# A layer step of a hybrid encoder on one core: the three shared projections loaded amid the modulation's weights and multiplied chunk by chunk

## The chip, the cores and the metric

The kernel runs on one core of a Trainium2 chip. The metric is device time in microseconds (us) of one execution. A core has a matrix engine, TensorE (PE; its weight loads are listed as PEld), VectorE (DVE), ScalarE (ACT), GpSimd (POOL) and SyncE (SP), whose queue (SPq) issues nearly all DMAs here. Each engine takes its instructions strictly in the order of its own queue; instructions of different engines wait for each other through semaphores.

## What is computed

One layer for two request groups that share weights: 256 prompt tokens and 8 x 16 sample tokens, 384 tokens of width 1024, in float32. The part that the change touches is the beginning:

```
mod = silu(c) @ w_ada + b_ada -> shift1, scale1, gate1, shift2, scale2, gate2   (per sequence, 9 sequences)
h   = RMSNorm(x) * (1 + scale1) + shift1
P   = h @ w_in        columns: [RWKV-7: r k v | wd ad gd] [attention: q k v qi ki wi] [two branch gates]
branch A: RWKV-7 time mixing on P (low-rank decay from tanh(wd), in-context rate from ad, gate from gd)
branch B: sparse attention with an indexer (qi, ki, wi) and top-k keys
m = sigmoid(gA) * (oA @ w_proj_a) + sigmoid(gB) * (oB @ w_proj_b);   x = x + gate1 * (m @ w_out)
h2 = RMSNorm(x) * (1 + scale2) + shift2;   x = x + gate2 * PEER(h2)     (product-key experts, 16,384 rows)
```

The "three shared projections" are the columns wd, ad and gd of w_in (96 to 128 columns each in the kernel's units wa, wb, wg): small inputs of the low-rank maps that all 16 RWKV heads share.

## The kernel before

The kernel is written with a tile framework: the program is traced in order, and a scheduler then lays down the order of every engine's queue from priorities (the order of tracing) and from a simulation of when each instruction's inputs are ready. Tiles come from pools; a pool that is opened in the memory of a closed one waits for the closed pool's readers. A tag with `bufs=n` has n buffers in turn, and a new tile waits until the buffer's last reader is done. The context `issue_after(ins)` places what is traced inside it, on `ins`'s engine, behind `ins` in that engine's queue.

**Precision.** A product in float32 quality is made of three matmuls: each operand is split into a high half (ScalarE copies to a rounded type, line 230) and a low half (VectorE or GpSimd subtracts, line 234), and high x high, high x low and low x high are summed in PSUM. `wload` (243) loads a weight unit and splits it; `raw` (236) is the load into one of four buffers of tag "w"; the high halves "wh" have four buffers, the low halves "wl" three (`WB = (4, 4, 3)`).

**The front** (`run`, 1585 ff., first pool "ph"):

- `setup` and `mod_head` load small constants; `front_x` (445) normalises three tiles of 128 tokens and transposes them into xT (8 chunks of 128 features x 384 tokens).
- `front_h` (463) goes over the 8 chunks two at a time. For chunks c, c+1 it needs two modulation units, `mod_unit(c // 2)` (shift) and `mod_unit(c // 2 + 4)` (scale). A unit (383) is 256 columns of w_ada: two loads of 512 KB, half a unit each; the matmuls of a half appear as eight instructions "mm<-w,cst", four transposing steps as "bx<-cfirst,mr" after ScalarE's copy "mr". Then VectorE makes h1A (404), VectorE and ScalarE modulate (480 to 484), and h is split into LTh (485, 486) and LTl (487 on VectorE for the sample tokens, 488 on GpSimd for the prompt).
- The units are traced in the order 0, 4, 1, 5, 2, 6, 3, 7: 16 loads of 512 KB.
- Line 1602 then loads wa, wb and wg (`self.early`) into buffers of tag "w", and behind the last of them in SP's queue come the late constants: cfront, clate, crope, a row of norm weights (qkn), the rope tables rt made on GpSimd (343 to 352) and six stores that clear DRAM scratch from a tile "zero" (357 to 365).

**What follows.** `rwkv_head` (515, pool "rw") calls `shifted` (491) for wa, wb and wg: it splits the weight, makes the whole product in a PSUM bank of tag "mm" (two banks; `tposp`, 276: 8 chunks x 3 terms = 24 matmuls), copies it to SBUF (502, 503), mixes each token with its forerunner, and from the results come XW (525), XV and XG. Then the work follows the string `ORDER` (177): two gate units (G, 24 matmuls each), the indexer (`index`, which begins with ki, 24 matmuls and a transposition in a "dx" bank), more gate units, the eight RWKV pairs (R), the other modulation units (M) and the attention quarters (D). The first use of XW on PE is the pair's decay product at line 561 ("fx<-XW,wup").

PSUM has eight banks: tags mm 2, fx 2, bx 1, dx 2, cp 1 (`PSB`). Up to `rwkv_head` the dx and cp banks are unused.

Of the kernel before, what the change touches and what calls it, by code (L numbers as in the profile page):

```python
# [18 lines left out]
OP = mybir.AluOpType  # L19
# [8 lines left out]
NT = 384  # L28


UNITS = {"wa": (3072, 128), "wb": (3200, 128), "wg": (3328, 96)}
# [164 lines left out]
class K:  # L196
# [58 lines left out]

    def win(self, name):
        n = UNITS[name][1]
        return self.wload(self.win_ap(name), n, self.early.pop(name, None)), n

    def win_ap(self, name):  # L260
        n = UNITS[name][1]
# [201 lines left out]
    def front_h(self):  # L463

        nc = self.nc
        hi = self.t([128, 8, NT], F32R, tag="LTh", pool=self.hpool)
        lo = self.t([128, 8, NT], F32R, tag="LTl", pool=self.hpool)
        self.LT = (hi, lo)
        self.h1B = self.scT[:, 0]
        self.h1A = self.pool.tile([128, 8, 9], F32, name="h1A")  # L470
        h = self.xT
        for c in range(0, 8, 2):
            cs = slice(c, c + 2)
            self.mod_unit(c // 2)
            self.mod_unit(c // 2 + 4)
            self.mod_cols(cs)
            hs = h[:, cs, 0:128]
            o = hs.rearrange("p c (b t) -> p c b t", t=16)
            bc = lambda a: a[:, cs, :8].unsqueeze(3).to_broadcast([128, 2, 8, 16])
            nc.vector.tensor_tensor(o, o, bc(self.h1A), op=OP.mult)  # L480
            nc.vector.tensor_tensor(o, o, bc(self.h1B), op=OP.add)
            for cc in (c, c + 1):
                hp = h[:, cc, 128:NT]
                nc.scalar.activation(hp, hp, AF.Identity, scale=self.h1A[:, cc, 8:9], bias=self.h1B[:, cc, 8:9])
            nc.scalar.activation(hi[:, cs, 0:128], hs, AF.Copy)
            nc.vector.tensor_copy(hi[:, cs, 128:NT], h[:, cs, 128:NT])
            nc.vector.tensor_tensor(lo[:, cs, 0:128], hs, hi[:, cs, 0:128], op=OP.subtract)
            nc.gpsimd.tensor_tensor(lo[:, cs, 128:NT], h[:, cs, 128:NT], hi[:, cs, 128:NT], op=OP.subtract)  # L488


    def shifted(self, name, ch, tag, bufs=2):

        nc = self.nc
        W, m = self.win(name)
        pt = self.t([128, 393], tag="pt", bufs=2)
        X = self.t([128, NT], tag=tag, bufs=bufs)
        pts = pt[:m, 0:136].rearrange("p (b t) -> p b t", t=17)
        ptp = pt[:m, 136:393]
        nc.gpsimd.tensor_copy(pts[:, :, 0], self.shT[:m, :, ch])
        nc.gpsimd.memset(ptp[:, 0:1], 0.0)  # L500
        p = self.tposp(W, 0, m, self.LT)
        nc.scalar.activation(pts[:, :, 1:], p[:, 0:128].rearrange("p (b t) -> p b t", t=16), AF.Copy)
        nc.scalar.activation(ptp[:, 1:], p[:, 128:NT], AF.Copy)
        Xs = X[:m, 0:128].rearrange("p (b t) -> p b t", t=16)
        Xp = X[:m, 128:NT]
        nc.gpsimd.tensor_tensor(Xs, pts[:, :, 0:16], pts[:, :, 1:17], op=OP.subtract)
        nc.gpsimd.tensor_tensor(Xp, ptp[:, 0:256], ptp[:, 1:257], op=OP.subtract)
        mu = self.col["mu"][:m, ch:ch + 1]
        nc.vector.scalar_tensor_tensor(Xs, Xs, mu, pts[:, :, 1:17], op0=OP.mult, op1=OP.add)
        nc.vector.scalar_tensor_tensor(Xp, Xp, mu, ptp[:, 1:257], op0=OP.mult, op1=OP.add)  # L510
        nc.gpsimd.tensor_copy(self.last[:m, 0:8, ch], pts[:, :, 16])
        nc.gpsimd.tensor_copy(self.last[:m, 8, ch:ch + 1], ptp[:, 256:257])
        return X
# [1071 lines left out]
    def run(self):  # L1585
        hs = self.ctx.enter_context(ExitStack())
        self.halves = self.open(hs, "halves")
        with ExitStack() as front:
            fh = front.enter_context(ExitStack())
            self.fconst = self.open(fh, "fconst")  # L1590
            self.hpool = self.open(fh, "hpool")
            self.fill = self.open(fh, "fill")
            self.psum = self.open(self.ctx, "psum", space=bass.MemoryType.PSUM)
            self.lo_pattern = "v"
            with ExitStack() as s:
                self.pool = self.open(s, "ph")
                self.setup()
                self.mod_head()
                self.front_x()
                self.front_h()  # L1600

                self.early = {name: self.raw(self.win_ap(name)) for name in ("wa", "wb", "wg")}
                with self.tc.issue_after(self.wdma.ins):
                    self.load_consts("cfront", self.fconst)
                    self.setup_front()
            self.lo_pattern = "v"
            self.gd = self.dt_([16, 128, NT])
            self.oad, self.obd = self.dt_([128, 8, NT]), self.dt_([128, 8, NT])
            with ExitStack() as s:
                rw = self.open(s, "rw")  # L1610
                self.pool = rw
                self.rwkv_head()
                self.rw = rw
                ds, n = None, dict.fromkeys("RGD", 0) | {"M": 8}
                for x in ORDER:
                    if x == "I":
                        with ExitStack() as s2:
                            self.pool = self.open(s2, "idx", side="right")
                            self.index()
                        ds = self.open(s, "dsa", side="right")  # L1620
                        continue
                    if x in "123":
                        self.pick_s() if x == "1" else self.pick_p("23".index(x))
                        continue
                    self.pool = rw if x == "R" else ds
                    self.lo_pattern = "g" if x == "g" else "v"
                    x = x.upper()
                    {"R": self.rwkv_pair, "M": self.mod_unit, "G": self.gate_unit, "D": self.dsa_quarter}[x](n[x])
                    n[x] += 1
                self.nc.sync.dma_start(self.O["sh"], self.last)  # L1630
            fh.close()
            self.hpool2 = self.open(self.ctx, "hpool2", side="right")
            qs = self.ctx.enter_context(ExitStack())
            self.qpool = self.open(qs, "qpool", side="right")
            with ExitStack() as s:
                mixp = self.pool = self.open(s, "mixp")
                self.mix()
                self.scores_head()
                for u in range(4):
                    self.out_unit(u)  # L1640
                sel = self.sel = self.open(qs, "sel", side="right")
                for i in range(3):
                    self.h2_tile(i)
# [49 lines left out]
        with ExitStack() as s:  # L1693
# [3 lines left out]
            nc = self.nc  # L1697
# [52 lines left out]
```

## Time and profile before

| | us |
|---|---|
| median of 3 runs | 1776.21 (1772.17 to 1779.79) |
| the profiled execution | 1770.59 |
| its span, first to last instruction | 1768.8 |
| PE busy in the span | 1672.8 |
| DVE / ACT / POOL busy | 1360.3 / 749.7 / 553.4 |

The mean granted clock of TensorE was 0.983 of full speed. In rows of the timeline the first number is the start in us from the span's start, the second the duration; then engine, line, operation, output and inputs, shapes, count, and in brackets the idle time before it and what ended it. Rows of the chain are start, duration, what. Rows of a table of stretches ("A:B") give the length, each engine's busy time with its count of instructions (PE, PEld, DVE, ACT, POOL), the granted TensorE clock, the DMA engines' busy share and GB/s. Matmuls are pipelined and their ends are modelled: the distance of two starts is the price of one in a row of them.

### The profile page before, as it was taken

The page shows a single profiled execution, that of the slowest core. Times are in us where ns is not written, and L with a number is a line of the kernel's source. Part 1 is how long each engine was busy: PE and PEld are TensorE (multiplying, and loading weights), DVE is VectorE, ACT ScalarE, POOL GpSimd, SP SyncE. Part 2 cuts the span into 40 slices and gives each one's busy share as a digit, 9 for nine tenths or more (in the row PEclk, how much of TensorE's full clock was granted, in tenths as well). Part 3 has the DMA queues.
Part 4 walks back from the last instruction along what each step waited for, and adds up shares of the span by engine and source line. Part 5 has one row for each costly group of instructions (what it writes and reads, how often), then busy time and mean ns, then how long its engine had stood idle before and what let it go on. Part 6 is the DMA issues. An engine that isn't in the chain of part 4 may idle for free.

```text
span 1768.8 us, 33168 instructions
## 1 busy us (share of the span) xinstructions
PE 1672.8 (95%) x12424; PEld 1402.2 (79%) x12424; DVE 1360.3 (77%) x2902; ACT 749.7 (42%) x1652; POOL 553.4 (31%) x616
## 2 busy tenths in 40 slices
PE   6999899999999999998989889999989999999998
PEld 4988688778888877998878789999966667667766
DVE  3448878778867765555999999899867777877787
ACT  4433343334243333334233265577853333443344
POOL 1433343333342320024032223242243333333332
PEclk8999899999999999999999989999999999999999
DMA  8543662555364365755388989987559999999995
GB/s 301 161 123 103 185 194 67 153 175 153 94 215 140 105 204 191 235 189 185 125 333 323 342 302 389 374 330 263 192 203 393 342 367 363 374 356 390 344 382 215
DMA packets 172537, 436.71 MB, mean 247 GB/s; under 512 B 46036, under 2 KB 86100, under 8 KB 155992
## 3 DMA queue, kind: packets, MB, share of 16 engines
q1 hardware_dynamic: 153944, 300.36, 50.5%
q0 software_dynamic: 18432, 134.23, 19.9%
q8 instruction: 98, 1.61, 0.4%
q14 instruction: 63, 0.52, 0.1%
HBM read 403.23 MB, written 31.30 MB: 246 GB/s over the span
## 4 chain that ended last, share of the span: by engine, by line
PE 55%; DVE 19%; DMA 14%; issue 6%; ACT 3%; POOL 2%; SPq 1%; DVEq 0%; POOLq 0%; ACTq 0%
PE mm L226 20%; PE fx L226 13%; PE dx L226 9%; PE cp L226 6%; PE bx L226 5%; DMA w<-in_pv 3%; DMA raw<-in_puv,pe 3%; DVE wl L234 3%; DVE acc L1581 2%; DVE raw L1575 2%; DMA w<-in_puT 2%; ACT wh L230 1%; DMA w<-in_w_ada 1%; DMA w<-in_w_in 1%; DMA NL<-d 1%
## 5 line engine op out<-in xcount | busy, mean ns | idle before, releaser
L234 DVE TENSOR_TENSOR wl<-w,wh 128x1024 fp32r<-128x1024 f32 (+1 forms) x280 | 351.7, 1263 | 108.4 <-ACT wh L230 72.4
L230 ACT ACTIVATE wh<-w 128x1024 fp32r<-128x1024 f32 (+1 forms) x288 | 300.8, 1051 | 171.6 <-PE mm L226 77.2
L1568 POOL DMA_INDIRECT raw<-in_puv,pe x128 | 171.2, 1338 | 446.6 <-PE dx L226 156.5
L226 PE MATMUL fx<-h2h,wl 128*128 128x256 f32 x736 | 209.6, 285 | 8.8 <-DVE wl L234 8.8
L226 PE MATMUL fx<-h2h,wh 128*128 128x256 f32 x736 | 210.3, 286 | 3.0 <-ACT wh L230 2.8
L226 PE MATMUL fx<-h2l,wh 128*128 128x256 f32 x736 | 207.3, 282 | 0.0
L1581 DVE SCALAR_TENSOR_TENSOR acc<-raw,dots,acc 128x1024 f32<-128x1024 f32 x127 | 165.6, 1304 | 16.0 <-ACT dots L1577 15.7
L1575 DVE SCALAR_TENSOR_TENSOR raw<-raw,sh 128x1024 f32<-128x1024 f32 x128 | 160.3, 1252 | 7.7 <-DMA raw<-in_puv,pe 7.5
L226 PEld LDWEIGHTS fx<-h2h,wl 128*128 128x128 f32 x736 | 139.9, 190 | 12.5 <-DVE wl L234 12.1
L226 PEld LDWEIGHTS fx<-h2h,wh 128*128 128x128 f32 x736 | 139.9, 190 | 7.8 <-ACT wh L230 6.3
L226 PEld LDWEIGHTS fx<-h2l,wh 128*128 128x128 f32 x736 | 139.9, 190 | 1.7 <-issue 1.3
L226 PE MATMUL fx<-h2f,w 128*128 128x256 f32 x576 | 128.2, 382 | 11.5 <-ACT G L1484 11.5
L226 PEld LDWEIGHTS fx<-h2f,w 128*128 128x128 f32 x576 | 108.1, 190 | 29.7 <-ACT G L1484 14.9
L226 PE MATMUL mm<-LTh,wh 128*128 128x384 f32 (+2 forms) x352 | 123.2, 351 | 1.9 <-ACT wh L230 1.3
L226 PE MATMUL mm<-LTl,wh 128*128 128x384 f32 (+2 forms) x352 | 122.7, 349 | 0.5 <-POOL LTl L488 0.5
L226 PE MATMUL mm<-LTh,wl 128*128 128x384 f32 (+2 forms) x352 | 122.1, 347 | 0.0
L226 PE MATMUL mm<-wh,LTh 128*128 128x256 f32 x336 | 99.2, 296 | 2.9 <-ACT qx L888 2.9
L226 PE MATMUL mm<-wl,LTh 128*128 128x256 f32 x336 | 98.5, 293 | 0.0
L226 PE MATMUL mm<-wh,LTl 128*128 128x256 f32 x336 | 97.7, 291 | 0.0
L1576 ACT ACTIVATE dots<-dots 128x1 f32<-128x1 f32 x128 | 25.5, 199 | 161.7 <-DVE raw L1575 159.3
L226 PEld LDWEIGHTS mm<-LTh,wh 128*128 128x128 f32 (+2 forms) x352 | 66.2, 188 | 7.7 <-issue 3.0
L226 PEld LDWEIGHTS mm<-LTl,wh 128*128 128x128 f32 (+2 forms) x352 | 66.3, 188 | 3.2 <-issue 1.5
(571 smaller groups left out, 4152.3 us busy)
## 6 DMA issues: line engine op xcount, KB each, us to landing
w<-in_puT SPq DMA_DIRECT2D x128, 512.0 KB
w<-in_pv SPq DMA_DIRECT2D x128, 512.0 KB
w<-in_w_in SPq DMA_DIRECT2D x70, 512.0 KB
w<-in_w_ada SPq DMA_DIRECT2D x48, 512.0 KB
cKT<-in_cKT SPq DMA_DIRECT2D x32, 256.0 KB
cV<-in_cV SPq DMA_DIRECT2D x32, 256.0 KB
w<-in_w_pq SPq DMA_DIRECT2D x16, 512.0 KB
d<-wst SPq DMA_DIRECT2D x8, 832.0 KB
```

The costliest lines, as they stand in the source:

```text
L226: return self.nc.tensor.matmul(out, l, r, start=start, stop=stop, skip_group_check=True, **kw)
L230: self.nc.scalar.activation(hi, src, AF.Copy)
L234: (self.nc.vector if eng == "v" else self.nc.gpsimd).tensor_tensor(lo, src, hi, op=OP.subtract)
L1568: d = nc.gpsimd.indirect_dma_start(out=bass.AP(tensor=u.tensor, offset=u.offset, ap=[u.ap[0], [1, 2048]]), out_offset=None, in_=self.I["puv"],
L1575: nc.vector.scalar_tensor_tensor(u, u, 1.0, h2, op0=OP.mult, op1=OP.mult, accum_out=dot)
L1576: nc.scalar.activation(dot, dot, AF.Gelu_apprx_tanh)
L1581: nc.vector.scalar_tensor_tensor(acc, v, dot, acc, op0=OP.mult, op1=OP.add)
```

## The change

The three weights wa, wb and wg are loaded behind the fourth modulation unit traced (unit 5, the eighth w_ada load) instead of behind the sixteenth, into three tiles of their own in the first pool, and are split there. Their products go to the two dx banks and the cp bank, open from then on: the matmuls of chunks 0 to 3 are traced after chunks 2 and 3 of h are split, those of 4, 5 and of 6, 7 after theirs. `shifted` takes the finished bank. The late constants are placed behind the last w_ada load on SP's queue and, what of them runs on GpSimd, behind the last LTl of h. The number of matmuls, splits and loaded bytes stays.

```diff
--- before.py
+++ after.py
@@ -255,7 +255,7 @@
 
     def win(self, name):
         n = UNITS[name][1]
-        return self.wload(self.win_ap(name), n, self.early.pop(name, None)), n
+        return self.wload(self.win_ap(name), n), n
 
     def win_ap(self, name):
         n = UNITS[name][1]
@@ -469,10 +469,14 @@
         self.h1B = self.scT[:, 0]
         self.h1A = self.pool.tile([128, 8, 9], F32, name="h1A")
         h = self.xT
+        self.first = {}
         for c in range(0, 8, 2):
             cs = slice(c, c + 2)
             self.mod_unit(c // 2)
             self.mod_unit(c // 2 + 4)
+            if c == 2:
+                with self.tc.issue_after(self.wdma.ins):
+                    self.first_weights()
             self.mod_cols(cs)
             hs = h[:, cs, 0:128]
             o = hs.rearrange("p c (b t) -> p c b t", t=16)
@@ -485,20 +489,45 @@
             nc.scalar.activation(hi[:, cs, 0:128], hs, AF.Copy)
             nc.vector.tensor_copy(hi[:, cs, 128:NT], h[:, cs, 128:NT])
             nc.vector.tensor_tensor(lo[:, cs, 0:128], hs, hi[:, cs, 0:128], op=OP.subtract)
-            nc.gpsimd.tensor_tensor(lo[:, cs, 128:NT], h[:, cs, 128:NT], hi[:, cs, 128:NT], op=OP.subtract)
+            self.lolast = nc.gpsimd.tensor_tensor(lo[:, cs, 128:NT], h[:, cs, 128:NT], hi[:, cs, 128:NT], op=OP.subtract)
+            for name in ("wa", "wb", "wg"):
+                if c == 2:
+                    self.first_products(name, (0, 1, 2, 3))
+                elif c > 2:
+                    self.first_products(name, (c, c + 1))
+
+    def first_weights(self):
+
+        for name, tag in (("wa", "dx"), ("wb", "dx"), ("wg", "cp")):
+            n = UNITS[name][1]
+            w = self.t([128, 1024], tag="we" + name)[:, :8 * n].rearrange("p (k c) -> p k c", k=8)
+            self.nc.sync.dma_start(w, self.win_ap(name))
+            self.first[name] = (self.wload(None, n, w), n, self.ps([128, NT], tag=tag)[:n])
+
+    def first_products(self, name, ks):
+
+        W, n, p = self.first[name]
+        hi, lo = self.LT
+        for k in ks:
+            wh, wl = W(k)
+            self.mm(p, wh, hi[:, k], start=(k == 0), stop=False)
+            self.mm(p, wh, lo[:, k], start=False, stop=False)
+            self.mm(p, wl, hi[:, k], start=False, stop=(k == 7))
 
 
     def shifted(self, name, ch, tag, bufs=2):
 
         nc = self.nc
-        W, m = self.win(name)
+        m = UNITS[name][1]
+        if name not in self.first:
+            W, m = self.win(name)
         pt = self.t([128, 393], tag="pt", bufs=2)
         X = self.t([128, NT], tag=tag, bufs=bufs)
         pts = pt[:m, 0:136].rearrange("p (b t) -> p b t", t=17)
         ptp = pt[:m, 136:393]
         nc.gpsimd.tensor_copy(pts[:, :, 0], self.shT[:m, :, ch])
         nc.gpsimd.memset(ptp[:, 0:1], 0.0)
-        p = self.tposp(W, 0, m, self.LT)
+        p = self.first[name][2] if name in self.first else self.tposp(W, 0, m, self.LT)
         nc.scalar.activation(pts[:, :, 1:], p[:, 0:128].rearrange("p (b t) -> p b t", t=16), AF.Copy)
         nc.scalar.activation(ptp[:, 1:], p[:, 128:NT], AF.Copy)
         Xs = X[:m, 0:128].rearrange("p (b t) -> p b t", t=16)
@@ -1599,8 +1628,7 @@
                 self.front_x()
                 self.front_h()
 
-                self.early = {name: self.raw(self.win_ap(name)) for name in ("wa", "wb", "wg")}
-                with self.tc.issue_after(self.wdma.ins):
+                with self.tc.issue_after(self.wdma.ins), self.tc.issue_after(self.lolast.ins):
                     self.load_consts("cfront", self.fconst)
                     self.setup_front()
             self.lo_pattern = "v"
```

## The prediction

> **What bounds the kernel now.** I read the engines' share of the chain, then a table of stretches, then the chain of the first 60 us, then each engine's rows there.
>
> ```profile
> PE 55%; DVE 19%; DMA 14%; issue 6%; ACT 3%; POOL 2%; SPq 1%; DVEq 0%; POOLq 0%; ACTq 0%
> ...
> 0.00:55.00 55.00, 38.53 (x255) 26.75 (x256) 22.71 (x56) 24.09 (x47) 17.21 (x41) 0.84 0.88 297
> ...
> sum 1768.00, PE 1672.83 PEld 1402.19 DVE 1360.28 ACT 749.73 POOL 553.39; mean PE 152.08 PEld 127.47 DVE 123.66 ACT 68.16 POOL 50.31
> ```
>
> The first number of each group is the engine's busy time. TensorE (PE) idles 1768.00 - 1672.83 = 95.2 us in all, and 55.00 - 38.53 = 16.5 us of that lies in the first 55 us: 1/32 of the span holds a sixth of the idle time. The chain says what the PE waits for there.
>
> ```profile
> 28.61 4.84 DMA w<-in_w_ada
> ...
> 35.10 6.04 DMA cfront<-in_cfront
> ...
> 47.10 1.25 POOL LTl L488
> ...
> 48.39 2.02 PE mm L226 x10
> ...
> 50.99 8.61 PE mm L226 x48
> ```
>
> Up to 36 us it is the w_ada loads; then the constants' loads, which hold SP's queue; then the last chunk of h's low half on POOL. From 48.39 on the chain is PE matmuls almost without a break, so the start of the matmuls is what the change can move, and a shift of that start reaches the end as long as nothing downstream is rearranged. I take as mark the first matmul of the first gate unit, G0, the first that belongs to none of the three shared products:
>
> ```profile
> 17.85 0.61 PE L226 MATMUL bx<-cfirst,mr 128*128 128x9 f32 x4
> ...
> 21.60 0.64 PE L226 MATMUL mm<-w,cst 128*32 128x256 f32 x8 [0.93 <-DMA w<-in_w_ada]
> ...
> 31.30 1.02 PE L226 MATMUL bx<-cfirst,mr 128*128 128x9 f32 x4
> ...
> 36.24 1.08 PE L226 MATMUL mm<-w,cst 128*32 128x256 f32 x8 [0.61 <-DMA w<-in_w_ada]
> ...
> 38.61 0.69 PE L226 MATMUL mm<-LTh,wh 128*128 128x384 f32 x1 [1.29 <-ACT wh L230]
> ...
> 40.59 0.52 PE L226 MATMUL mm<-LTh,wh 128*128 128x384 f32 x1
> ...
> 40.91 0.52 PE L226 MATMUL mm<-LTl,wh 128*128 128x384 f32 x1
> ...
> 43.53 0.34 PE L226 MATMUL mm<-LTh,wl 128*128 128x384 f32 x1
> ...
> 43.70 0.34 PE L226 MATMUL mm<-LTh,wh 128*128 128x384 f32 x1
> ...
> 55.27 0.34 PE L226 MATMUL mm<-LTh,wh 128*128 128x384 f32 x1
> ...
> 59.52 0.92 PE L226 MATMUL fx<-XW,wup 64*128 64x384 f32 x4
> ```
>
> G0 starts at 55.27. The same rows give the prices of PE work at two clocks. A product matmul starts 0.32 us after its forerunner at 40.59 to 40.91 (cold) and 0.17 to 0.18 us at 43.53 to 43.70 (warm; I use 0.175). Half a modulation unit (one row "mm<-w,cst" x8) takes 0.64 warm, 1.08 cold; its transposing step (bx x4) 0.61 and 1.02. The row at 21.60 is the 8th half unit of 16, the one at 36.24 the 16th.
>
> **The change, part by part.** No matmul, split or byte is added or removed; 72 product matmuls (3 names, 8 chunks, 3 terms) and three loads change place.
>
> *The loads.* The three weights move from behind the 16th w_ada load to behind the 8th.
>
> ```profile
> 20.00:30.00 10.00, 6.61 (x68) 3.03 (x59) 3.08 (x10) 4.07 (x10) 2.76 (x2) 0.79 0.91 317
> 30.00:40.00 10.00, 7.84 (x54) 4.25 (x46) 4.54 (x9) 4.43 (x9) 1.26 (x1) 0.50 0.95 313
> ...
> w<-in_w_in SPq DMA_DIRECT2D x21, 512.0 KB
> w<-in_w_ada SPq DMA_DIRECT2D x16, 512.0 KB
> ...
> w<-in_w_in SPq DMA_DIRECT2D x1, 384.0 KB
> ```
>
> The last three numbers of a window are granted clock, DMA share and GB/s: the DMA engines are 91 to 95% busy, so bytes put in front delay what follows. wa and wb are 512 KB each, wg 384 KB (the one load of that size): 1.44 MB, at 315 GB/s 4.6 us. The 16th half unit, which waited for its load until 36.24, starts at 40.8. That is the cost. SP issues these loads without a buffer wait (they get tiles of their own), so the w_ada loads behind them stand only in the line of bytes.
>
> *The last chunk of h.* What is saved is seen by comparing the third chunk's chain with the last one's.
>
> ```profile
> 25.82 1.38 POOL L488 TENSOR_TENSOR LTl<-xT,LTh 128x512 fp32r<-128x512 f32 x1 [2.58 <-DVE LTh L486]
> ...
> 30.65 0.39 ACT L392 ACTIVATE mr<-mm 128x256 f32<-128x256 f32 x1 [2.95 <-PE mm L226]
> ...
> 34.42 1.26 POOL L488 TENSOR_TENSOR LTl<-xT,LTh 128x512 fp32r<-128x512 f32 x1 [7.21 <-DVE LTh L486]
> ...
> 38.47 0.37 ACT L392 ACTIVATE mr<-mm 128x256 f32<-128x256 f32 x1
> 38.59 2.51 DVE L234 TENSOR_TENSOR wl<-w,wh 128x1024 fp32r<-128x1024 f32 x2 [2.54 <-ACT wh L230]
> ...
> 42.72 0.16 DVE L404 SCALAR_TENSOR_TENSOR h1A<-scT,cols 128x18 f32<-128x18 f32 x1
> ...
> 43.89 3.21 POOL L352 TENSOR_TENSOR rt<-rt,qkn 128x96 f32<-128x96 f32 x8
> ...
> 44.04 0.52 DVE L486 CAST LTh<-xT 128x512 fp32r<-128x512 f32 x1 [0.24 <-ACT xT L484]
> ...
> 47.06 1.28 POOL L488 TENSOR_TENSOR LTl<-xT,LTh 128x512 fp32r<-128x512 f32 x1
> ```
>
> Third chunk: from its copy mr at 30.65 to the end of LTl at 34.42 + 1.26 = 35.68 is 5.03 us. Last chunk: mr begins at 38.47, 1.15 after the 16th half unit's end (36.24 + 1.08), and LTl ends at 48.34, 9.87 after mr. So 1.15 + 9.87 - 5.03 = 6.0 us are stalls: mr behind a split on ACT, h1A behind wl on DVE, LTl behind the eight rt products on POOL (LTh is done at 44.56, LTl starts 2.5 later). All their causes move: the splits to about 24 to 29 us, where these engines idle, and the rt products, which are now queued behind this LTl. If the splits ran late, up to 3.5 of the 6.0 would come back.
>
> So h is complete at 40.8 + 1.08 + 0.1 + 5.03 = 47.0. Then only chunks 6 and 7 of three products remain, 18 x 0.175 = 3.15: **G0 at 50.2 by loads and chain**, 49.3 if the half unit and its transposing step run warm (0.44 + 0.41 less).
>
> *The PE's own work* is the other bound. The second chunk's LTl ends at 25.82 + 1.38 = 27.2, and no early product can start before it. The weights are there by then: wa lands one load after 21.60, at 23.3, wg at about 26.2; the three low halves, 1.25 each on DVE (2.51 for two), end near 28 to 29. From 27.2 the PE must do 8 half units, 4 transposing steps and 72 products before G0: warm 8 x 0.64 + 4 x 0.61 + 72 x 0.175 = 20.2; cold half units and steps add 5.2.
>
> ```profile
> 28.00:30.00 2.00, 2.00 (x20) 1.13 (x12) 0.18 (x1) 0.00 (x0) 0.00 (x0) 0.50 1.01 350
> ...
> 42.00:44.00 2.00, 2.00 (x11) 2.00 (x10) 1.73 (x6) 1.08 (x3) 1.80 (x5) 0.80 0.99 237
> ```
>
> The granted clock is 0.50 here and comes back inside 42 to 44; a mean of 0.80 puts that at 42.8, 4.2 us after the dense product matmuls begin at 38.61. So I charge the first 4 us of early products cold: 12 matmuls, 12 x 0.145 = 1.8 more. That gives **27.2 + 20.2 + 1.8 = 49.2** with modulation warm and **54.4** with all of it cold. [...]
>
> I take the middle: half the modulation work (halves 9 to 12) stands ahead of the early products and is cold, half behind them and is warm: G0 at 51.8. Against 55.27 that is **3.5 us saved**. The loads-and-chain bound (50.2) lies under it, so the PE, newly filled, is what is late next.
>
> *The constants and the zero stores* go behind the last LTl. Nobody on the PE's path waits for them directly; the price is in the second rival. *The banks*: wa and wb take both dx banks and wg takes cp; the next dx user is ki's transposition, three units of 24 matmuls (12.6 us) after G0's start. *The wl buffers*: there are three, all held by the shared weights until their last chunk, so G0's low half cannot be written before wa's last matmul, 1.05 us into the 3.15; 1.25 on DVE ends 0.85 before G0 is due. No cost, and no early start for G0 either.
>
> **Sum.** The profiled run took 1770.59 us (span 1768.8 and 1.8 around it); minus 3.5 is 1767.1. The median of the runs shown is 1776.21, 5.6 above the profiled one; I keep that distance: **1772.7 us**. By the ends 49.2 and 54.4 it is 1770.1 to 1775.3.
>
> **The rivals.**
>
> *Slower: the early products run cold.* Place: PE, 27 to 47 us. If the mixture with modulation work never brings the clock back, 54 products cost 0.32 each (17.3) and modulation 12.7; with the last 18 warm, G0 comes at 27.2 + 17.3 + 12.7 + 3.15 = 60.4, 5.1 late: 1781.3. The delay also frees the w buffers late. It decides once G0 passes 55.27: all modulation cold (54.4) and six more products cold. For: the row of 28 to 30, fully busy at 0.50. Against: 38.61 to 42.8, where product matmuls among a modulation step did release it. Chance 0.17.
>
> *Slower or no gain: the next pool opens late.*
>
> ```profile
> SPq L520 <- POOL LTl L488: 2.5, 1, 2.5
> ...
> 41.16 1.08 SPq L365 DMA_DIRECT2D d<-zero  x2
> ...
> 42.20 0.57 POOL L343 COPY rt<-crope 128x96 f32<-128x96 f32 x1 [6.52 <-DMA crope<-in_crope]
> ...
> 48.37 0.33 SPq L520 DMA_DIRECT2D shT<-in_shT  x1
> ...
> 53.85 0.53 ACT L525 ACTIVATE XW<-XW 64x384 f32<-64x384 f32 x1 [1.35 <-DVE XW L510]
> ```
>
> shT, a tile of the RWKV pool, waited for LTl, a reader of the first pool. Now the first pool's last work is the rt block (42.20 to 47.10, 4.9), the clearing of zero and six stores at 0.54, all behind LTl, and a landing (some 2.5, an estimate from shT's three). With h complete at 48.6 the RWKV pool opens near 59.7, and XW, ready at 54.38 or 6.0 after shT's issue, near 65.7. If the decay product (59.52) keeps its place behind G0, the PE stalls 6.2: 1782.4. If it stands behind G1 and ki, nothing is lost; the queues are planned with these dependencies known, so I give the stall 0.15.
>
> *More gained: the order behind is laid anew.* Each queue's order comes from a simulation, which sees the front change by some us. Some 79 us of PE idle time lie behind 55 us; a tenth more or less of it is 8 us: 1764.7 on the good side, about 1780.7 on the bad, which falls together with the other rivals. Nothing in the profile says which. Chance of the good side 0.21.
>
> **How the numbers follow.** Forecast (1770.1 to 1775.3) 0.47, cold 0.17, late pool 0.15, more gained 0.21. A measurement of this kernel can tell about 0.5%, 8.9 us, from no change. Faster by that needs 1767.3 or less: nearly all of "more gained", 0.19. Slower needs 1785.1: two of the slow cases together, or a downstream loss on top of one, 0.11. The rest, 0.70, is no change that can be told. The range 1764 to 1783 takes in the forecast, the cold and the late-pool case and most of "more gained"; it leaves out about 0.08 below and 0.10 above.
>
> **What would show it.** Right: the 16th w_ada half unit starts at 40 to 42 and the last LTl ends 5 to 6 us after it; product matmuls stand between 27 and 46; 18 matmuls lie between that LTl and G0; G0 starts at 50 to 54; the clock is 1.00 by about 36. Wrong: w_ada loads that wait for a buffer because the PE is busy with products (the 16th starting after 44), 0.50 up to 46, the decay product waiting for XW, or a G0 shift that isn't found again at the end.

## The result, and the profile after

The changed kernel is slower. Its median is 1787.35 us (5 runs, 1782.46 to 1791.42) against 1775.12 us of the kernel before beside it (5 runs, 1772.17 to 1779.79): a ratio of 1.0053, 95% interval 1.0030 to 1.0076. The ratio is an estimate of its own and lies below the quotient of the two medians: by it the loss is 9.4 us, by the medians 12.2. The forecast of 1772.7 us and its range up to 1783 were missed on the slow side. The profiled execution took 1783.0 us, its span 1781.2.

The engines' share of the chain, and the first 55 us as a row of a table of stretches, after (the columns are those of the rows of before):

```profile
PE 57%; DVE 20%; DMA 12%; issue 4%; ACT 3%; POOL 2%; SPq 1%; DVEq 0%; POOLq 0%; ACTq 0%
```

```profile
0.00:55.00 55.00, 38.98 (x268) 27.86 (x269) 20.62 (x52) 23.36 (x41) 13.36 (x24) 0.91 0.80 272
```

PE's busy time in the first 55 us hardly moved (38.98 for 38.53), though the first gate unit now starts before their end. The front, in PE's timeline after:

```profile
22.29 0.64 PE L226 MATMUL mm<-w,cst 128*32 128x256 f32 x8 [2.03 <-DMA w<-in_w_ada]
...
24.93 0.69 PE L226 MATMUL dx<-LTh,wh 128*128 128x384 f32 x1 [0.52 <-ACT wh L230]
...
31.13 0.52 PE L226 MATMUL dx<-LTl,wh 128*128 128x384 f32 x1
31.45 0.38 PE L226 MATMUL dx<-LTh,wl 128*128 128x384 f32 x1
...
35.90 0.34 PE L226 MATMUL cp<-LTh,wl 128*96 128x384 f32 x1
...
42.97 1.08 PE L226 MATMUL mm<-w,cst 128*32 128x256 f32 x8 [0.23 <-DMA w<-in_w_ada]
...
49.83 0.45 PE L226 MATMUL mm<-LTh,wh 128*128 128x384 f32 x1 [1.47 <-ACT wh L230]
...
53.43 0.34 PE L226 MATMUL mm<-LTh,wh 128*128 128x384 f32 x1
```

The eighth half unit stands at 22.29, the early products of chunks 0 to 3 run from 24.93 to 35.90, the sixteenth half unit is at 42.97. The row at 49.83 is the first of two matmuls of G0 that have slipped ahead of the last 18 products of the shared projections; G0 proper goes on at 53.43. Against 55.27 that is 1.84 us earlier: the gain that the change is made of was there, in this pair of profiles at about half the size. The place scatters between executions: in the seven profiles with the front of before (the profile shown ahead and those of six experiments below) G0 starts at 54.36 to 56.93, 55.4 on the mean.

It is gone 20 us later, behind this wait of PE on ScalarE (row of after):

```profile
74.45 0.39 PE L226 MATMUL mm<-wh,LTh 128*128 128x256 f32 x1 [1.67 <-ACT qx L917]
```

And the 12.4 us by which the spans differ (1781.2 - 1768.8) arise where nothing was edited. Both kernels do 12,424 matmuls. From 78 to 317 us and again from 700 us to the end the queues of the changed kernel hold the same instructions in the same order as before's, but for two ScalarE instructions near 1422 us that have changed places. Between 317 and 700 us the order differs. The table of stretches, cut at the same two PE instructions in both kernels; first before, then after:

```profile
0.00:315.83 315.83, 290.07 (x2397) 243.41 (x2397) 207.52 (x528) 123.73 (x266) 108.36 (x189) 0.96 0.53 162
315.83:696.76 380.93, 368.87 (x4233) 308.87 (x4231) 285.51 (x744) 138.09 (x334) 122.88 (x174) 0.99 0.53 161
696.76:1768.80 1072.04, 1013.89 (x5800) 849.90 (x5799) 867.24 (x1631) 487.90 (x1052) 322.15 (x253) 0.99 0.82 302
```

```profile
0.00:318.58 318.58, 292.24 (x2397) 245.74 (x2397) 208.26 (x531) 123.74 (x266) 111.48 (x189) 0.95 0.52 161
318.58:706.97 388.39, 377.39 (x4231) 310.90 (x4231) 285.55 (x740) 138.29 (x334) 116.71 (x174) 0.99 0.50 153
706.97:1781.20 1074.23, 1014.46 (x5800) 852.55 (x5799) 866.35 (x1633) 487.68 (x1052) 309.76 (x253) 0.99 0.83 303
```

The three parts differ by +2.8, +7.5 and +2.2 us. The middle one, which begins 260 us behind the last edited instruction, carries most. Its idle time did not grow: 380.93 - 368.87 = 12.1 us before, 388.39 - 377.39 = 11.0 after. What grew is PE's *busy* time, for the same matmuls at the same granted clock (0.99). Ends of matmuls are modelled, so a wait of a few tenths between two of them can show as busy. The starts don't have that fault: of the 4,230 distances from one matmul's start to the next one's in this stretch, 364 were over 0.20 and at most 0.50 us before and 400 after, and they took 92.9 and 102.7 us; all others took 288.1 and 285.7.

The two digits of the granted clock hide short losses. In the traces' clock record TensorE stands at half clock for 27.3 us of the first part before and 31.1 after, for 26.2 and 29.4 us of the last part, and for 6.8 and 6.5 us of the middle one. If half of that time is lost (an estimate: 128x384 products stand 0.32 us apart at a granted clock of 0.50 and 0.17 to 0.18 at 1.00), the clock accounts for 1.9 of the +2.8 us and 1.6 of the +2.2, and for none of the +7.5.

### The profile page after: what moved, and what is told of

Same layout as the page of the kernel before. It is cut to its first block, busy times and chain, and to the rows that moved or that the text cites. A ratio compares the mean times of both kernels' runs of the same rounds, so it can differ in the third digit from the quotient of the medians.

```text
span 1781.2 us, 33153 instructions
## 1 busy us (share of the span) xinstructions
PE 1684.1 (95%) x12424; PEld 1409.2 (79%) x12424; DVE 1360.2 (76%) x2902; ACT 749.7 (42%) x1652; POOL 538.0 (30%) x616
## 3 DMA queue, kind: packets, MB, share of 16 engines
q1 hardware_dynamic: 153944, 300.36, 50.2%
## 4 chain that ended last, share of the span: by engine, by line
PE 57%; DVE 20%; DMA 12%; issue 4%; ACT 3%; POOL 2%; SPq 1%; DVEq 0%; POOLq 0%; ACTq 0%
PE mm L226 20%; PE fx L226 13%; PE dx L226 10%; PE cp L226 7%; PE bx L226 6%; DVE wl L234 3%; DMA w<-in_pv 3%; DVE raw L1604 2%; DVE acc L1610 2%; DMA w<-in_puT 2%; ACT wh L230 2%; DMA raw<-in_puv,pe 2%; DMA NL<-d 1%; DVE TX L727 1%; DMA d<-MBp 1%
## 5 line engine op out<-in xcount | busy, mean ns | idle before, releaser
L234 DVE TENSOR_TENSOR wl<-w,wh 128x1024 fp32r<-128x1024 f32 x277 | 352.1, 1280 | 114.0 <-ACT wh L230 70.9
L230 ACT ACTIVATE wh<-w 128x1024 fp32r<-128x1024 f32 x285 | 297.7, 1051 | 182.9 <-PE mm L226 85.1
L226 PE MATMUL mm<-LTh,wh 128*128 128x384 f32 (+1 forms) x328 | 114.0, 347 | 1.5 <-ACT wh L230 1.5
L226 PE MATMUL mm<-LTl,wh 128*128 128x384 f32 (+1 forms) x328 | 114.3, 348 | 0.0
L226 PE MATMUL mm<-LTh,wl 128*128 128x384 f32 (+1 forms) x328 | 113.6, 347 | 0.0
L226 PEld LDWEIGHTS mm<-wh,LTh 128*128 128x128 f32 x336 | 65.4, 195 | 10.0 <-ACT qx L917 7.1
L226 PEld LDWEIGHTS mm<-wl,LTh 128*128 128x128 f32 x336 | 65.6, 195 | 2.2 <-issue 1.4
```

The costliest lines, as they stand in the source:

```text
L226: return self.nc.tensor.matmul(out, l, r, start=start, stop=stop, skip_group_check=True, **kw)
L230: self.nc.scalar.activation(hi, src, AF.Copy)
L234: (self.nc.vector if eng == "v" else self.nc.gpsimd).tensor_tensor(lo, src, hi, op=OP.subtract)
```

## The experiments

Twelve kernels ran, each beside the kernel before on the same chip (its median was 1776.7 to 1777.3 us there). A ratio is to the kernel before; its 95% interval stands in brackets.

### Front and order taken apart

**The theory** after the result: the planner (the framework's scheduler), seeing a front that differs by a microsecond or two, laid the queues of 317 to 700 us anew, and that order is the slower one. **The rival**: the new front itself costs the time (late buffers, late constants), and the order is innocent. To part them, an order was written into the kernel. Every instruction behind about 90 us gets an edge to its forerunner in its own queue; such an edge only fixes the order of one queue, it adds no semaphore and no instruction:

```diff
+    def hold_order(self):
+        for e, (skip, text) in HELD.items():
...
+            for x, y in zip(seq, seq[1:]):
+                self.tc.add_manual_dep(y.ins, x.ins.name, mybir.DependencyInfo(
+                    mybir.DependencyClass.NoSync, mybir.DependencyReason.DATA), reason="held")
```

One kernel has the front of before with the downstream order of after:

> Nothing of the change is in this kernel: its front is that of before. Only the order of the queues behind about 90 us is held to the one that the changed kernel got (it differs between 317 and 700 us). Theory 'order laid anew': +7 to +12 us against before, G0 at 55.3 as before, the stages level with before up to 317 us and the difference arising between 317 and 700. Rival 'the new front costs it': within 2 us of before. Third: about half (+4), if drifts in stages of equal order make the rest.

Measured: 1.0052 (1.0031 to 1.0073), 9.2 us and the changed kernel's ratio again, with nothing of the change in it. The other has the whole change with the order of before:

> The whole change, but the queues behind about 90 us keep the order of before. Theory 'order laid anew': -1 to +3.5 us against before, level with it from 80 us on. Rival 'the new front costs it': +10 to +12 as the changed kernel. Third: +4 to +6, from stages of equal order that drift by the clock (near 200 and 825 us).

Measured: 1.0004 (0.9985 to 1.0023). The crossing is clean: the time goes with the order, not with the front. The two orders part at 316 us on VectorE and 317 on TensorE. The first place on ScalarE shows how small such a difference is. In before, then with the order of after:

```profile
321.16 0.85 ACT L947 ACTIVATE rpt<-qx 128x768 f32<-128x768 f32 x1
321.91 1.04 ACT L230 ACTIVATE wh<-w 128x1024 fp32r<-128x1024 f32 x1
```

```profile
321.57 1.06 ACT L270 ACTIVATE wh<-w 128x1024 fp32r<-128x1024 f32 x1 [2.01 <-DMA w<-in_w_in]
322.53 0.83 ACT L987 ACTIVATE rpt<-qx 128x768 f32<-128x768 f32 x1
```

A square of an attention quarter and the split of the next weight unit have changed places; here the split waits 2.01 us for its load, with the square queued behind it.

Does it take the whole change to tip the planner, and do the held edges themselves cost anything? The kernel before with a single extra GpSimd operation, nothing held, answers both:

```diff
                 self.front_h()
+                self.nc.gpsimd.tensor_tensor(self.LT[1][:, 6:8, 128:NT], self.xT[:, 6:8, 128:NT], self.LT[0][:, 6:8, 128:NT], op=OP.subtract)
```

> The kernel before, nothing held, with one redundant GpSimd operation behind front_h: LTl of the last two chunks, prompt half, is written a second time (the same values, 1.3 us on POOL). The planner answers with the downstream order of the changed kernel. Theory 'order laid anew': G0 at most 1.5 us later than in before and the end +7 to +12 us, the difference again arising between 317 and 700 us; it also shows that the held order in the other runs is not what costs. Rival 'only the changed front costs it': +0 to +1.5.

Measured: 1.0060 (1.0034 to 1.0086). 1.3 us of work on an engine that is a third busy, and by the ratio the end comes 10.7 us later. Between 317 and 700 us its queues hold the order of the changed kernel; nothing else of the change is in it, and no held edge. The control for the edges, before held to its own order:

> The kernel before, its queues behind about 90 us held to the very order that they have: the instructions and their order are the same. Theory: holding costs nothing, within 0.2% of before. Its profile is a second profile of before as well: where it differs from the first by a step in a stage of equal order (such steps of 1.5 to 4.5 us stood near 200 and near 825 us in the others), that step belongs to the execution and not to the kernel. Rival: the holding itself costs some us, and the held runs were all too slow by that.

Measured: 1.0015 (0.9992 to 1.0039): nothing that can be told. Its profile is worth as much. It has before's instructions in before's order, and still its three parts are 317.09, 377.52 and 1071.79 us long against 315.83, 380.93 and 1072.04. So a part of one profile carries 3 us and more that belong to the execution. The +2.8 and +2.2 at the two sides of the changed kernel's middle part are of that size and say nothing, and one pair of profiles could not carry the +7.5 either. The middle part in six further kernels, with the order of before in the first two and that of after in the next two; the last two follow below:

```profile
317.09:694.61 377.52, 366.77 (x4231) 307.10 (x4231) 285.31 (x743) 138.16 (x334) 123.03 (x174) 1.00 0.52 163
```

```profile
319.96:703.53 383.57, 370.13 (x4231) 309.56 (x4231) 285.56 (x742) 138.59 (x334) 123.58 (x174) 0.99 0.53 160
```

```profile
314.42:702.84 388.42, 377.80 (x4231) 310.79 (x4231) 287.51 (x743) 138.24 (x334) 117.20 (x174) 0.99 0.50 154
```

```profile
322.15:713.68 391.53, 379.75 (x4231) 313.21 (x4231) 286.73 (x740) 137.88 (x334) 118.36 (x174) 0.99 0.50 152
```

Seven profiles with the order of before lie between 377.5 and 384.5 us, three with that of after between 388.4 and 391.5. Much of the scatter within the groups is the clock: TensorE is at half clock for 2.5 to 10.7 us of this part. With half of that time taken off (the estimate as above) the seven lie between 376.0 and 379.6 us and the three between 385.1 and 386.2.

Where in the order is it? Near 472 us both orders have done the same set of instructions on every engine, so they can be spliced there:

> The front of before; the queues follow the order of the changed kernel from 317 to 472 us (where both orders have done the same set of instructions on every engine) and that of before from there on. Theory: the loss is spread over the new order, as the stage times of before_front_after_order have it (-1.5 at 300, +2.6 at 475, +4.6 at 700): +3 to +5 here. Rival: it is one bad place in the second part: within 2 of before.

> The other half: the order of before up to 472 us, that of the changed kernel from there to 700. Theory (spread): +2 to +5, and the two halves together make what before_front_after_order made. Rival (one bad place in the second part): +6 to +10.

Measured: 1.0034 (1.0014 to 1.0055) and 1.0039 (1.0022 to 1.0056), 6.0 and 6.9 us, each a little more than expected, and in the middle part:

```profile
318.68:705.57 386.89, 372.73 (x4232) 310.47 (x4231) 287.08 (x741) 137.87 (x334) 121.92 (x174) 0.99 0.50 159
```

```profile
317.70:703.51 385.81, 375.17 (x4231) 310.70 (x4231) 285.45 (x741) 139.07 (x334) 118.58 (x174) 0.99 0.50 155
```

Both halves cost. The 6.9 us of the second half alone would suit the rival of one bad place there, but that rival wanted the first half within 2 us of before, and it costs 6.0. The sum of the two, 1.0073, is the upper end of the interval of the whole. So the loss does not sit in one place. Which of the several hundred swaps matter stays open.

Is the order of before a lucky one, that any new order must lose to? Two more orders, those that the planner lays for two parts of the change alone, on the front of before:

> The front of before; the queues behind about 90 us are held to a third order, the one that the planner lays for the change without its early loads (weights loaded behind the sixteenth w_ada load, products in the idle banks). It parts from the order of before from about 260 to 700 us. If the order of before is one of the lucky ones, this one is slower too: +4 to +12. If the orders scatter around that of before, it is as likely faster: -8 to +8. No way to work out a number from the traces.

> The front of before; the queues are held to a fourth order, the one that the planner lays when only the late constants are moved behind the last LTl. It parts from the order of before from about 100 to 850 us. The same two readings as for the third order: +4 to +12 if the order of before is a lucky one, -8 to +8 if orders scatter around it.

Measured: 1.0010 (0.9992 to 1.0029) and 1.0017 (0.9994 to 1.0040): no sign that the order of before is a lucky one. Of four orders three can't be told apart and one is half a per cent slower. The change met that one.

The third order also tests the count of short distances. Its middle part:

```profile
316.27:699.33 383.06, 374.55 (x4233) 311.90 (x4231) 285.15 (x743) 139.21 (x334) 115.63 (x174) 0.99 0.51 156
```

Distances over 0.20 and at most 0.50 us number 360 to 378 in the seven profiles with the order of before and 400 to 425 in the three with that of after. But there are 395 and 397 in the two spliced kernels, which lose only a part, and 410 in the third order, where PE's busy time is high too and its idle time is 8.5 us. So the count goes with a re-laid order and is not shown to be what makes it slow.

### Where the front's own gain went

With the order of before held, the whole change gives 1.0004, so its front is worth nothing that can be measured either. G0 starts 1.8 to 3.1 us earlier than in the profile of before (53.43 after, 52.21 with the order held), 2.6 on the means, and by the first transposition of the q units (PE's "dx<-cfirst,qr") the gain has gone: 76.94 and 77.54 against 77.05 in before. (With before's front that transposition stands between 76.14 and 78.71 in the seven profiles, 77.2 on the mean.) The suspect was the late pool. Rows after of SP, of ScalarE and of PE:

```profile
53.08 1.25 SPq L365 DMA_DIRECT2D d<-zero  x2
...
56.38 0.33 SPq L549 DMA_DIRECT2D shT<-in_shT  x1
```

```profile
48.72 1.06 ACT L230 ACTIVATE wh<-w 128x1024 fp32r<-128x1024 f32 x1 [1.51 <-DMA w<-in_w_in]
49.68 0.40 ACT L489 ACTIVATE LTh<-xT 128x256 fp32r<-128x256 f32 x1
...
56.41 0.28 ACT L531 ACTIVATE pt<-dx 128x128 f32<-128x128 f32 x1 [1.90 <-DMA d<-zero]
```

```profile
65.42 0.33 PE L226 MATMUL mm<-LTh,wl 128*72 128x384 f32 x1
65.68 0.92 PE L226 MATMUL fx<-XW,wup 64*128 64x384 f32 x4
```

The RWKV pool waits for the six stores of "zero" and opens at 56.4 us. The finished shared products sit in their banks until then. Their post-processing, begun at 56.41 instead of 50.41, then meets the sigmoids and exponentials of the first pair on ScalarE, and qx is copied late: that is the theory for the 1.67 us at 74.45. Also to be seen: the last LTh on ScalarE stands behind G0's weight split, which waited 1.51 us for its load. The first cure puts the rope block and the tile "zero" into a pool of their own:

```diff
-        z = self.t([128, 520], tag="zero")
+        z = self.t([128, 520], tag="zero", pool=self.tail)
```

> As after_front_before_order, and besides the rope block, its constant and the tile that clears scratch lie in a pool of their own, so that the RWKV pool's memory waits for the last LTl alone. Theory 'late pool': shT is issued at 49 to 51 us instead of 56.4, the first tile of the RWKV pool on ACT no longer waits for a zero store, the PE's 1.67 us stall behind qx near 74 us goes, and from 80 us on it is 1.5 to 2 us ahead of after_front_before_order. Rival: the crowding of ACT is only moved, no difference from 80 us on.

Measured: 1.0005 (0.9984 to 1.0025). shT is issued at 50.35, and the 1.67 us are gone. But:

```profile
54.32 0.31 ACT L622 ACTIVATE guh<-gup 128x128 fp32r<-128x128 f32 x1 [4.51 <-DMA gup<-in_gup]
54.54 0.29 ACT L625 ACTIVATE guh<-gup 96x128 fp32r<-96x128 f32 x1
54.74 1.04 ACT L270 ACTIVATE wh<-w 128x1024 fp32r<-128x1024 f32 x1
```

```profile
55.83 0.44 PE L266 MATMUL mm<-LTh,wh 128*128 128x384 f32 x1 [2.49 <-ACT wh L270]
```

With the pool open early, the first pair's small splits become ready early and are queued ahead of a weight split that the gate units need: PE waits 2.49 us at 55.83, and the q transposition stands at 77.71. The theory was right about the stall and wrong about the gain; the crowd only moved, as the rival had it. The next kernel also took on the other two losses: the products that hold the PE while half units wait (below), and the LTh behind G0's split (G0's split and matmuls placed behind the last LTh and the last shared product):

```diff
-                if c == 2:
-                    self.first_products(name, (0, 1, 2, 3))
-                elif c > 2:
-                    self.first_products(name, (c, c + 1))
+                if c == 6:
+                    self.first_products(name, range(8))
```

> As after_tail_pool, and besides (a) the early products of all eight chunks are traced behind chunk 6, so that modulation units go ahead of them wherever both are ready, and (b) G0's weight split on ACT stands behind the last LTh and G0's matmuls behind the last shared product. Theory: no hole in the w_ada loads at 30 to 40 us (DMA share over 0.8 instead of 0.48), 16th half unit at 40 to 41 instead of 42.97, last LTh 1.5 to 2 us earlier relative to it, G0 at 50.5 to 52 instead of 53.4; 3 to 5 us ahead of before from 80 us on, and as much at the end if nothing else drifts. Rival: the products then pile up behind the last half unit and run cold, G0 at 54 or later, no gain.

Measured: 1.0019 (1.0000 to 1.0039). The sixteenth half unit is at 41.12, h is complete at 47.93 instead of 50.53 and G0 starts at 52.33, but the same small splits now delay G0's low half: its first low-half matmul waits 2.08 us for wl and stands at 55.77. The DMA share at 30 to 40 us rose from 0.48 to 0.65 only, not to the 0.8 expected. Next, these splits behind the second gate unit's:

> As after_units_first (order of before held), and besides the first pair's gup splits stand behind the second gate unit's weight split on ACT and on DVE. Theory: in after_tail_pool and after_units_first G0 lost its gain because these splits, ready early with the early pool, went ahead of G0's; now G0 starts at 52.3 or earlier and its low-half product does not wait for wl (2.08 us there), so that it is 2.5 to 3.5 us ahead of before from 80 us on, and as much at the end. Rival: the gain goes again to the crowding of ACT behind qx near 74 us (1.67 in the changed kernel): 0.5 to 1.5 us ahead at 80.

Measured: 1.0008 (0.9985 to 1.0030). G0's first matmul is at 52.04, as expected, and neither reading saw what comes next. PE waits longer than in any other kernel's first 85 us, in rows of PE, DVE and POOL:

```profile
56.89 0.45 PE L266 MATMUL mm<-LTh,wl 128*128 128x384 f32 x1 [3.99 <-DVE wl L274]
```

```profile
50.55 7.42 DVE L274 TENSOR_TENSOR wl<-w,wh 128x1024 fp32r<-128x1024 f32 x2 [2.51 <-issue]
```

```profile
50.32 2.14 POOL L392 TENSOR_TENSOR rt<-rt,qkn 128x96 f32<-128x96 f32 x6
52.41 0.32 POOL L566 COPY pt<-shT 128x8 f32<-128x8 f32 x2
52.69 0.72 POOL L392 TENSOR_TENSOR rt<-rt,qkn 128x96 f32<-128x96 f32 x2
...
54.51 0.18 POOL L579 COPY last<-pt 128x1 f32<-128x1 f32 x1
...
55.70 1.17 POOL L579 COPY last<-pt 128x1 f32<-128x1 f32 x1
```

Two wl subtractions, 1.22 us each on the median of before, take 7.42: the first one alone stands from 50.55 to 56.83, while GpSimd runs one short operation after another. The last kernel moves only the rope operations that begin this row:

```diff
                 self.rwkv_head()
+                with self.tc.issue_after(self.plast.ins):
+                    self.setup_rope()
```

> As after_best_front, with one block moved: the rope tables rt (12 operations on POOL) stand behind the shared projections' post-processing instead of directly behind the last LTl. Theory: in after_best_front one wl of G0 took 6.28 us on DVE instead of 1.22, beside an unbroken row of POOL operations that began with these; with them gone it takes 1.2 to 2, G0's low-half product no longer waits (3.99 us there), the first product of G0 stays near 52.0, and the kernel is 2.5 to 3.5 us ahead of before from 80 us on. Rival: the wait belongs to something else (wl's buffer or its DMA) and stays at 2 us or more.

Measured: the pair of wl takes 2.36 us again,

```profile
51.12 2.36 DVE L274 TENSOR_TENSOR wl<-w,wh 128x1024 fp32r<-128x1024 f32 x2 [4.00 <-issue]
```

G0 starts at 52.60 and doesn't wait, and the first q transposition comes at 75.33, 0.8 to 3.4 us ahead of the seven profiles with before's front and 1.8 ahead of their mean. This is about half of the gain that was forecast for the change, and it took five further edits and a held order to keep it. At the end it is 0.9998 (0.9977 to 1.0018), 1775.48 us: the best version found, by the two ratios 0.5% faster than the changed kernel, and not to be told from the one before. Some 2 us are 0.1%, which this measurement doesn't resolve.

## Why the prediction was wrong, point by point

**The step that failed** is in one sentence of the first part: "a shift of that start reaches the end as long as nothing downstream is rearranged". Something was: the order of 317 to 700 us, which alone costs 1.0052, some 9 us. The rival for it was named and even sized ("a tenth more or less of it is 8 us", measured 7.5 in the profile and 9 in the ratio), but only its good side got a chance; the bad side was said to fall together with other rivals and got none of its own. Nothing in the profile favoured either sign, so the two sides should have had equal chances, and "slower by over 0.5%" more than 0.11. That the size fits is luck: it was a tenth of PE's idle time, and the idle time of the middle part did not grow (12.1 before, 11.0 after); the loss shows as busy time.

**The loads.** The sixteenth half unit was forecast at 40.8 and came at 42.97. The forecast's bytes are the first part. The rest is the case that it named as "w_ada loads that wait for a buffer because the PE is busy with products" and that its sum left out: there the w_ada loads "stand only in the line of bytes". The stretch after, and SP's longest wait of the front:

```profile
30.00:40.00 10.00, 9.73 (x76) 7.22 (x74) 0.95 (x5) 1.15 (x3) 0.00 (x0) 0.92 0.48 128
...
SPq L240 <- PE mm L226: 18.8, 11, 4.9
```

PE was busy 9.73 of 10 us, and the loads fell from 313 to 128 GB/s. In the second row, of 10 to 60 us, SP waits 18.8 us for PE in 11 waits; the longest, 4.9 us, ends at 37.94, at the issue of the last w_ada load but one.

**The last chunk of h.** From the half unit's end to the last LTl 5.13 us were forecast (47.0 less 41.88). It took 6.5: DVE's LTl ends at 50.53, behind ScalarE's LTh, which stood behind G0's split (48.72 and 49.68 above):

```profile
50.11 0.42 DVE L491 TENSOR_TENSOR LTl<-xT,LTh 128x256 fp32r<-128x256 f32 x1 [2.44 <-ACT LTh L489]
```

The stalls named in the prediction were gone; one it did not name was late next. A step moved away from an engine's queue lets something else of a later stage move up. With the late half unit (2.2) and this (1.4) h was 3.5 us late, and G0 came 2.9 us after it. So the bound by loads and chain, given as 50.2 and as lying under the PE's own work, was the one that held, at 53.4: it was undersized by 3.2 us.

**The clock.** Forecast: cold for the first 4 us of early products, 1.00 by 36. The products are 0.32 apart until 31.45 and 0.17 to 0.18 after it, so it came back 6.5 us after 24.93, with half units among the products (granted 0.50 in 26 to 30, 0.62 in 30 to 32, 1.00 in 32 to 40); and it was lost again, since the half units at 41.68 and 42.97 take 1.06 and 1.08 (0.50 in 42 to 44). The rival in which it never comes back (G0 at 60.4) did not come true; G0 at 53.43 lies inside the bounds 49.2 to 54.4. The size of 3.5 us was too high by 1.7 in this pair of profiles, because h was late. The 1.47 us that PE stood before G0's matmul at 49.83 are part of that: the last 18 shared products all needed the LTh that ended at 50.08.

**The late pool.** XW was forecast near 65.7 for a pool that opens near 59.7; the pool opened at 56.4, and the decay product came at 65.68, with no wait ahead of it. That the two times agree is luck: the product was laid behind the ki unit, the harmless variant. The price came another way, through ScalarE (1.67 us at 74.45), which the prediction did not follow: it asked who waits for XW, and not what else the late work would meet.

**The wl buffers** were given "no cost". In the changed kernel that held: G0's first low-half matmul, at 53.77, did not wait. In two later kernels with an earlier G0 it did, 2.08 and 3.99 us, but for small splits ahead of the subtraction and for a slow subtraction, not for a buffer.

Not shown: whether the 3 us between the 12 us of the changed kernel's medians and the 9 us of its order alone are anything; the intervals overlap widely. Of the 12.4 us between the two profiled spans, 3.3 would be the clock by the estimate above.

## What to carry to other kernels

Where a planner lays the queues, an edit of a microsecond is two edits: itself, and a new draw of the order of everything behind it, which here cost up to 0.6%, several times what the edit itself moved. (Of three re-laid orders one cost that much, two cost nothing that can be told, and none gained.) Compare such an edit with the later order held fast, or give both signs of the draw equal chances and a range to match. And a gain at the head of a kernel is only as good as the next queue that the work meets: look at what moves up into each gap that the edit opens, engine by engine.

## What was not expected of the hardware

One DVE subtraction of 128x1024 f32 with both operands in SBUF took 6.28 us instead of 1.22 beside an unbroken row of 19 GpSimd operations of 0.1 to 0.6 us, and 1.2 again (2.36 for two) when the row began later. The GpSimd operation that follows the row, from 55.70, took 1.17 us where the same one had taken 0.18 at 54.51, and it ended with the subtraction, at 56.87 and 56.83; this would fit a subtraction that ran only then, which no run shows by itself. The reverse is in the changed kernel: the eight rt products took 5.31 us beside three such subtractions (3.72 for the three), and 3.21 in before, beside none. So in one kernel the DVE operation was the one drawn out and in the other the GpSimd operations were; what decides it, and why one subtraction stood over nineteen short operations, no run shows.
